# Experts' up products over both parts of the tokens at once, in an encoder layer with a mixture of experts

## Chip, cores and metric

One core of a Trainium2 chip runs one program. The metric is the device time of one execution in microseconds; the times shown are medians of several runs. TensorE (PE) multiplies matrices into PSUM, VectorE (DVE), ScalarE (ACT) and GpSimd (POOL) work beside it, SyncE (SP) issues most of the DMA.

## What is computed

One layer: a normalisation, a projection, neighbourhood attention beside a convolution, an output projection with a residual, then a mixture of 16 experts in which each expert chooses 256 of the 2048 tokens, and a last normalisation. The change is in the experts:

```python
def expert_choice_ffn(h, w_router, w_gate, w_up, w_down):
    logits = jnp.einsum('bsd,de->bse', h, w_router, preferred_element_type=jnp.float32)
    aff = jax.nn.softmax(logits, axis=-1)
    gates, idx = lax.top_k(jnp.swapaxes(aff, 1, 2), cap)      # cap = 256
    xs = h[bidx, idx]
    hid = jax.nn.silu(jnp.einsum('becd,edf->becf', xs, w_gate)) * jnp.einsum('becd,edf->becf', xs, w_up)
    eo = jnp.einsum('becf,efd->becd', hid, w_down)
    return jnp.zeros_like(h).at[bidx, idx].add(gates[..., None].astype(h.dtype) * eo)
```

The model width is 1024, an expert's hidden width 2048, everything is float32.

## The kernel before

A float32 matrix is multiplied as two parts: a high part, which is the value rounded to the matmul's format (fp32r), and a low part, which is what is left. `split` (L122) makes them: ScalarE copies the value into the high part (L123), VectorE subtracts that from the value for the low part (L124). A product of two such matrices is three matmuls, high by high, high by low and low by high; `mm3` issues them one after the other, all through `mm` (L103).

**Experts.** The loop at the end of the kernel goes over 257 chunks. A chunk `jj` is expert `e` and `j` of 16, 128 of the 2048 hidden columns. `up_chunk` makes both up products (`i` = 0 with `w_gate`, 1 with `w_up`) in the two halves of one PSUM bank: for each of 8 slices `d` of the model width, three matmuls whose stationary operand is 128x128 of the weights (`wh` or `wl`) and whose moving operand is one part of the 256 tokens (`xh` or `xl`). `act_chunk` takes Silu of the first half on ScalarE (L1037), multiplies it by the second half on VectorE (L1038), both out of PSUM, and splits the result into `hid`. `down_chunk` multiplies the `hid` of the chunk before by `w_down`, 12 matmuls of 512 columns, into four banks (`accs`) that stay for all 16 chunks of an expert. Behind it stand the jobs of the table `todo`, and then three of the six splits of the next weights, 128x1024 each (`split_part`).

**What stands around it.** The rows of an expert's tokens are gathered by DMA and `turn` transposes them: for `b` = 0 to 3, four transposes (L106) into one bank and a split into the high and the low part of slices 2b and 2b+1. Turns 0 and 1 of the next expert stand in `todo` of an expert's fifteenth chunk, turns 2 and 3 in that of its last, so that they come right ahead of the next expert's first `up_chunk`. In chunks 0 to 26 `todo` also holds the routing of the experts 1 to 15, a search for the affinity of the 256th token: each step takes the last count, offers candidates and reduces on VectorE (L887 to L876), and TensorE counts (a small matmul from `rd`, in the table `early`, between the up products and the down product of the next chunk). One-hot tables (L953) and their lists follow. At an expert's first chunk `finish_expert` scales the sums of the one before (ScalarE L1064, VectorE L1066).

**Order and buffers.** Each engine executes its instructions in the order in which they are written (`manual_schedule`); semaphores stand where one needs another's result or buffer. PSUM has eight banks: four for `accs`, four that rotate. Small tiles of up to 2 KB a partition come from 8 buffers (`e2`), large ones of 8 KB from 22 slots.

Of the kernel before, what the change touches and what calls it, by code (L numbers as in the profile page):

```python
# [9 lines left out]
F32R = mybir.dt.float32r  # L10
BF16 = mybir.dt.bfloat16
I32 = mybir.dt.int32
AF = mybir.ActivationFunctionType
ALU = mybir.AluOpType
AX = mybir.AxisListType

P = 128
# [3 lines left out]
E = 16  # L21
# [33 lines left out]
def kernel(  # L55
# [16 lines left out]
    nc = tc.nc  # L72
# [11 lines left out]
    def uid(s):  # L84
        counter[0] += 1
        return f"{s}{counter[0]}"

    def slot(shape, dt=F32):
        return big.tile(shape, dt, tag="s", name=uid("s"))

    def e2(shape, dt=F32):
        return sm.tile(shape, dt, tag="e2", name=uid("e"))
# [4 lines left out]
    def bank(shape, dt=F32):  # L97
        return psum.tile(shape, dt, tag="b", name=uid("b"))

    pe = [None]  # L100

    def mm(o, l, r, start, stop):
        pe[0] = nc.tensor.matmul(o, l, r, start=start, stop=stop)  # L103

    def tr(o, i, idt):
        pe[0] = nc.tensor.transpose(o, i, idt)  # L106
# [9 lines left out]
    def mm3(o, lh, ll, rh, rl, start, stop):  # L116

        mm(o, lh, rh, start, False)
        mm(o, lh, rl, False, False)
        mm(o, ll, rh, False, stop)  # L120

    def split(hi, lo, src):  # L122
        nc.scalar.activation(hi, src, AF.Copy)  # L123
        nc.vector.tensor_tensor(lo, src, hi.bitcast(F32), op=ALU.subtract)  # L124
# [292 lines left out]
    u = slot([P, T])  # L417
# [13 lines left out]
    for n, (kind, i) in enumerate(jobs):  # L431
# [3 lines left out]
        if kind == "a":  # L435
            u = slot([P, T])
# [333 lines left out]
    for k, b in enumerate((2, 3, 0, 1)):  # L770
        on((98, 106, 112, 118)[k], lambda b=b: wo_load(b))
        for n in range(4):
            i = (104, 109, 115, 121)[k] + n
# [12 lines left out]
    for i in range(-LS, NT_):  # L786
# [5 lines left out]
        j = i + LS  # L792
        if j < NT_:
            h, k = divmod(j, 16)
# [179 lines left out]
    xs_raw, xsT = {}, {}  # L974
# [11 lines left out]

    def turn(e, b):
        if b == 0:
            xsT[e] = (slot([P, 8, 256], F32R), slot([P, 8, 256], F32R))
        hi, lo = xsT[e]  # L990
        ps = bank([P, 2, 256])
        for hf in range(2):
            for j in range(2):
                d = b * 2 + j
                tr(ps[:, j, hf * P : (hf + 1) * P], xs_raw[e][:, hf, d * P : (d + 1) * P], ident)
        split(hi[:, b * 2 : b * 2 + 2], lo[:, b * 2 : b * 2 + 2], ps)


    raw_w, hl_w = {}, {}
# [12 lines left out]
    def split_part(u, part, k):  # L1012

        if k == 0:
            shape = [P, 8, 256] if part < 2 else [P, 2, D]
            hl_w[u, part] = (slot(shape, F32R), slot(shape, F32R))
        split(*(v.rearrange("p a b -> p (a b)")[:, k * 1024 : (k + 1) * 1024] for v in (*hl_w[u, part], raw_w[u, part])))
        if k == 1 and 0 < u < NU - 2:
            load_part(u + 2, part)
# [1 line left out]
    hid = {}  # L1021
    accs = {}

    def up_chunk(e, j):
        u = e * 8 + j // 2
        xh, xl = xsT[e]
        fs = slice((j % 2) * P, (j % 2 + 1) * P)
        ps = bank([P, 2, 256])
        for i in range(2):
            wh, wl = hl_w[u, i]  # L1030
            for d in range(8):
                mm3(ps[:, i], wh[:, d, fs], wl[:, d, fs], xh[:, d], xl[:, d], d == 0, d == 7)
        return ps

    def act_chunk(e, j, ps):
        s = e2([P, 256])
        nc.scalar.activation(s, ps[:, 0], AF.Silu)  # L1037
        nc.vector.tensor_tensor(s, s, ps[:, 1], op=ALU.mult)  # L1038
        h = e2([P, 2, 256], F32R)
        split(h[:, 0], h[:, 1], s)  # L1040
        hid[e, j] = h

    def down_chunk(e, j):
        if j == 0:
            accs[e] = [bank([P, 512]) for _ in range(4)]
        h = hid.pop((e, j))
        wh, wl = hl_w[e * 8 + j // 2, 2]
        for m in range(2):
            ms = slice(m * P, (m + 1) * P)
            for n in range(2):  # L1050
                ns = slice(n * 512, (n + 1) * 512)
                mm3(
                    accs[e][m * 2 + n], h[:, 0, ms], h[:, 1, ms], wh[:, j % 2, ns], wl[:, j % 2, ns],
                    j == 0, j == 15,
                )
# [84 lines left out]
    for b in range(4):  # L1140
        turn(0, b)
# [41 lines left out]
    for e in range(1, E):  # L1183
        j = (e - 1) * 16 + {1: 9, 2: 10}.get(e, 4)
# [7 lines left out]
    for t in range(16):  # L1192
        j = (E - 1) * 16 + 2 + t * 3 // 4
# [4 lines left out]
    for jj in range(E * 16 + 1):  # L1198
        e, j = divmod(jj, 16)
        u = jj // 2  # L1200
        ps = up_chunk(e, j) if e < E else None
        for f in early.pop(jj, []):
            f()
        if e < E:
            act_chunk(e, j, ps)
        if jj:
            down_chunk(*divmod(jj - 1, 16))
            if j == 0 and e < E:
                finish_expert(e - 1)
        if e == E:  # L1210
            break
        for f in todo.pop(jj, []):
            f()
        if u + 1 < NU:
            for p_, k in order[(j % 2) * 3 : (j % 2) * 3 + 3]:
                split_part(u + 1, p_, k)

    e = E - 1
# [114 lines left out]
```

## Time and profile before

| | us |
|---|---|
| median of 3 runs (3258.41 to 3263.06) | 3260.43 |
| the profiled execution | 3264.74 |
| its span, first to last instruction | 3263.0 |
| PE busy (share of the span) | 3137.8 (96%) |
| DVE busy | 2082.9 (64%) |
| ACT busy | 1368.9 (42%) |
| POOL busy | 500.8 (15%) |

The first 1025 us of the span are projections, attention, convolution and the router, the rest are the experts. Matmuls are pipelined: the next starts before one has ended, so that the pace of a stream is read from starts, or from the length of a merged row: its length holds one duration and, for each further matmul, one step of the pace. A row of the order of time merges instructions of one group that follow each other on an engine; a figure in brackets is the idle time ahead of it and what ended it.

### The profile page before, as it was taken

What the parts mean: (1) busy time and instruction counts of PE and PEld (TensorE: products, weight loads), DVE (VectorE), ACT (ScalarE), POOL (GpSimd) and SP (SyncE); (2) the same over time, 40 slices, a digit from 0 to 9 for tenths busy, and PEclk for the clock granted to TensorE, in tenths of its full rate; (3) what the DMA queues carried; (4) which work ended last, traced back from release to release, by engine and by line L of the source; (5) the groups of instructions that cost most, each with busy time, mean ns of one, the idle gap of its engine ahead of it and who ended that gap; (6) DMA issues with size and microseconds to landing.
All of it is one profiled execution on the core that took longest, in us unless ns stands there. A gap on an engine that the chain in (4) does not pass through costs nothing.

```text
span 3263.0 us, 51574 instructions
## 1 busy us (share of the span) xinstructions
PE 3137.8 (96%) x21282; PEld 2880.2 (88%) x21282; DVE 2082.9 (64%) x3229; ACT 1368.9 (42%) x2248; POOL 500.8 (15%) x358
## 2 busy tenths in 40 slices
PE   7999997869997999999999999999999999999998
PEld 6888976767886999999999999999999999999997
DVE  5799966786766787555556555555555555555565
ACT  5111126753333444444444444444444444444454
POOL 2111116665541000000000000000000000000011
PEclk9999998988997999999999999999999999999999
DMA  6231379972334565655656566565665656556585
GB/s 252 59 96 64 121 189 228 225 211 96 124 132 170 203 194 181 212 189 195 205 194 202 191 204 197 188 203 197 198 202 195 195 191 213 189 194 205 194 283 201
DMA packets 392923, 602.51 MB, mean 185 GB/s; under 512 B 13936, under 2 KB 316272, under 8 KB 388976
## 3 DMA queue, kind: packets, MB, share of 16 engines
q1 hardware_dynamic: 357552, 550.91, 51.6%
q0 software_dynamic: 9504, 34.61, 4.2%
q10 hardware_dynamic: 25632, 13.70, 1.4%
q8 instruction: 167, 2.74, 0.3%
q14 instruction: 68, 0.56, 0.1%
HBM read 527.86 MB, written 71.30 MB: 184 GB/s over the span
## 4 chain that ended last, share of the span: by engine, by line
PE 86%; DMA 5%; DVE 5%; issue 2%; POOL 1%; SPq 1%; ACT 0%; POOLq 0%; ACTq 0%; DVEq 0%
PE b L103 83%; DVE s L272 3%; PE b L106 2%; DMA s<-kl_scr 2%; DMA s<-in_tb_dram 1%; DMA s<-v_scr 1%; SPq L110 1%; POOL e L533 0%; POOL s L483 0%; PE b L573 0%; DMA s<-kh_scr 0%; DMA s<-in_xT_dram 0%; DMA gains<-in_rows_dram 0%; DVE s L488 0%; DVE e L124 0%
## 5 line engine op out<-in xcount | busy, mean ns | idle before, releaser
L103 PE MATMUL b<-s,s 128*128 128x256 f32 (+1 forms) x15616 | 2247.5, 302 | 25.9 <-DMA s<-kl_scr 17.5
L103 PEld LDWEIGHTS b<-s,s 128*128 128x128 f32 x15616 | 2073.8, 192 | 138.9 <-issue 18.9
L124 DVE TENSOR_TENSOR s<-s,s 128x1024 fp32r<-128x1024 f32 x768 | 896.3, 1220 | 116.3 <-ACT s L123 106.4
L123 ACT ACTIVATE s<-s 128x1024 fp32r<-128x1024 f32 x768 | 754.8, 1045 | 35.4 <-issue 31.5
L103 PE MATMUL b<-s,e 128*128 128x512 f32 x3072 | 746.7, 392 | 0.0
L103 PEld LDWEIGHTS b<-s,e 128*128 128x128 f32 x3072 | 560.6, 189 | 105.6
L1037 ACT ACTIVATE e<-b 128x256 f32<-128x256 f32 x256 | 98.3, 384 | 986.8 <-PE b L103 986.8
L1038 DVE TENSOR_TENSOR e<-e,b 128x256 f32<-128x256 f32 x256 | 107.7, 421 | 578.4 <-ACT e L1037 578.3
L272 DVE SCALAR_TENSOR_TENSOR s<-s,pv_sb,s 128x2033 f32<-128x2033 f32 (+14 forms) x120 | 310.4, 2587 | 2.0
L1067 POOL DMA_INDIRECT acc<-s,c x30 | 55.7, 1857 | 1251.4 <-ACT s L1064 1141.2
L124 DVE TENSOR_TENSOR e<-e,e 128x256 fp32r<-128x256 f32 x256 | 108.7, 425 | 123.8 <-ACT e L123 123.8
L978 POOL DMA_INDIRECT s<-h_scr,c x32 | 55.7, 1742 | 763.1 <-issue 498.2
L533 POOL TENSOR_SCALAR e<-e,c 128x384 f32<-128x384 f32 (+2 forms) x114 | 143.8, 1269 | 130.5 <-DVE c L531 58.1
L123 ACT ACTIVATE e<-e 128x256 fp32r<-128x256 f32 x256 | 106.9, 417 | 130.0 <-DVE e L1038 130.0
L521 ACT ACTIVATE e<-e,c 128x384 f32<-128x384 f32 (+2 forms) x128 | 79.4, 621 | 92.1 <-DVE c L531 75.0
L573 PE MATMUL b<-s,s 128*128 128x256 f32 (+3 forms) x512 | 96.3, 310 | 18.4 <-DVE s L560 18.2
L573 PEld LDWEIGHTS b<-s,s 128*128 128x128 f32 (+1 forms) x512 | 88.0, 216 | 26.8 <-DVE s L560 22.7
L106 PE MATMUL b<-ident,e 128*96 128x128 f32 (+1 forms) x448 | 81.6, 304 | 30.1 <-POOL e L533 29.9
L517 DVE CUSTOM_DVE_ANT_0 e<-b,s 128x384 f32<-128x384 f32 (+2 forms) x128 | 71.1, 555 | 52.1 <-DMA s<-in_tb_dram 34.7
L124 DVE TENSOR_TENSOR s<-b,s 128x512 fp32r<-128x512 f32 x80 | 52.5, 688 | 70.4 <-ACT s L123 70.3
L106 PEld LDWEIGHTS b<-ident,e 128*96 128x96 f32 (+1 forms) x448 | 52.6, 144 | 41.0 <-POOL e L533 38.5
L560 DVE TENSOR_TENSOR s<-b,s 128x384 fp32r<-128x384 f32 (+3 forms) x128 | 78.3, 612 | 15.9 <-ACT s L555 11.8
(139 smaller groups left out, 1485.3 us busy)
## 6 DMA issues: line engine op xcount, KB each, us to landing
s<-in_w_gate_dram SPq DMA_DIRECT2D x128, 1024.0 KB
s<-in_w_up_dram SPq DMA_DIRECT2D x128, 1024.0 KB
s<-in_w_down_dram SPq DMA_DIRECT2D x128, 1024.0 KB
s<-in_x_dram SPq DMA_DIRECT2D x8, 1024.0 KB
s<-in_xT_dram SPq DMA_DIRECT2D x8, 1024.0 KB
v_scr<-e ACTq DMA_DIRECT2D x32, 256.0 KB
s<-kh_scr SPq DMA_DIRECT2D x16, 512.0 KB
s<-kl_scr SPq DMA_DIRECT2D x16, 512.0 KB
```

What stands on the lines that cost most here:

```text
L103: pe[0] = nc.tensor.matmul(o, l, r, start=start, stop=stop)
L106: pe[0] = nc.tensor.transpose(o, i, idt)
L123: nc.scalar.activation(hi, src, AF.Copy)
L124: nc.vector.tensor_tensor(lo, src, hi.bitcast(F32), op=ALU.subtract)
L272: nc.vector.scalar_tensor_tensor(a[:, s:e], u[:, s + sh : e + sh], tap_w(k), a[:, s:e], op0=ALU.mult, op1=ALU.add)
L517: nc.vector.tensor_tensor_reduce(out=s[:, :n], in0=ps[:, :n], in1=bt[:, boff : boff + n], scale=-1.0, scalar=3.0e38, op0=ALU.add, op1=ALU. ...
L521: nc.scalar.activation(s[:, :n], s[:, :n], AF.Exp, bias=nm[:, rg : rg + 1], scale=-1.0, accum_out=rs_[:, rg : rg + 1])
L533: eng.tensor_scalar(s[:, :n], s[:, :n], ri, None, op0=ALU.mult)
L560: nc.vector.tensor_tensor(lo, src, hi.bitcast(F32), op=ALU.subtract)
L573: nc_mm = nc.tensor.matmul(o[:, r0 : r0 + nr], vt[:nk, g], part[:nk, at : at + nr], start=g == 0 and p == 0, stop=g == 7 and p == 1, skip_ ...
L1037: nc.scalar.activation(s, ps[:, 0], AF.Silu)
L1038: nc.vector.tensor_tensor(s, s, ps[:, 1], op=ALU.mult)
```

## The change

The tokens' parts now lie beside each other: `xsT` is two tiles of four slices each, and in a slice the 256 values of the high part are followed by the 256 of the low part. `up_chunk` makes one of the two up products in a bank of its own. Eight matmuls in a row take a slice of the weights' high part against both parts of the tokens, 512 columns, into both halves of the bank; eight more take the weights' low part against the tokens' high part, 256 columns, into the first half. The new `sum_chunk` adds the halves: ScalarE copies the second into an `e2` tile, VectorE adds the first to it. `act_chunk` then works from these tiles and no longer from PSUM. In `turn` the split writes into strided halves of a tile, with the same number of instructions. The count of columns that TensorE streams is the same.

```diff
     def turn(e, b):
         if b == 0:
-            xsT[e] = (slot([P, 8, 256], F32R), slot([P, 8, 256], F32R))
-        hi, lo = xsT[e]
+
+            xsT[e] = [slot([P, 4, 2, 256], F32R) for _ in range(2)]
+        hi, lo = (xsT[e][b // 2][:, 2 * (b % 2) : 2 * (b % 2) + 2, k] for k in range(2))
...
-        split(hi[:, b * 2 : b * 2 + 2], lo[:, b * 2 : b * 2 + 2], ps)
+        split(hi, lo, ps)
...
-    def up_chunk(e, j):
-        u = e * 8 + j // 2
-        xh, xl = xsT[e]
+    def up_chunk(e, j, i):
+
+        wh, wl = hl_w[e * 8 + j // 2, i]
         fs = slice((j % 2) * P, (j % 2 + 1) * P)
         ps = bank([P, 2, 256])
-        for i in range(2):
-            wh, wl = hl_w[u, i]
-            for d in range(8):
-                mm3(ps[:, i], wh[:, d, fs], wl[:, d, fs], xh[:, d], xl[:, d], d == 0, d == 7)
+        for d in range(8):
+            x2 = xsT[e][d // 4][:, d % 4]
+            nc.tensor.matmul(ps, wh[:, d, fs], x2, start=d == 0, stop=False, skip_group_check=True)
+        for d in range(8):
+            xh = xsT[e][d // 4][:, d % 4, 0]
+            pe[0] = nc.tensor.matmul(ps[:, 0], wl[:, d, fs], xh, start=False, stop=d == 7, skip_group_check=True)
         return ps
 
-    def act_chunk(e, j, ps):
-        s = e2([P, 256])
-        nc.scalar.activation(s, ps[:, 0], AF.Silu)
-        nc.vector.tensor_tensor(s, s, ps[:, 1], op=ALU.mult)
+    def sum_chunk(ps):
+
+        s = e2([P, 2, 256])
+        nc.scalar.activation(s[:, 0], ps[:, 1], AF.Copy)
+        nc.vector.tensor_tensor(s[:, 1], ps[:, 0], s[:, 0], op=ALU.add)
+        return s
+
+    def act_chunk(e, j, g, u):
+        nc.scalar.activation(g[:, 0], g[:, 1], AF.Silu)
+        nc.vector.tensor_tensor(g[:, 0], g[:, 0], u[:, 1], op=ALU.mult)
         h = e2([P, 2, 256], F32R)
-        split(h[:, 0], h[:, 1], s)
+        split(h[:, 0], h[:, 1], g[:, 0])
         hid[e, j] = h
...
-        ps = up_chunk(e, j) if e < E else None
+        if e < E:
+            g = sum_chunk(up_chunk(e, j, 0))
+            u2 = sum_chunk(up_chunk(e, j, 1))
         for f in early.pop(jj, []):
             f()
         if e < E:
-            act_chunk(e, j, ps)
+            act_chunk(e, j, g, u2)
```

How the rows then stand. On TensorE, in the first chunk of expert 0, before: the last slice `d` of the first up product and the first slice of the second. `b_` is the PSUM bank's tile; behind the arrow stand the moving operand (`s_9167` the tokens' high part, `s_9168` their low part) and the stationary one (`s_9046` and `s_9047` the two parts of `w_gate`, `s_9155` and `s_9156` those of `w_up`):

```order
L103 MATMUL b_9205<-s_9167,s_9046 128x256
L103 MATMUL b_9205<-s_9168,s_9046 128x256
L103 MATMUL b_9205<-s_9167,s_9047 128x256
L103 MATMUL b_9205<-s_9167,s_9155 128x256
L103 MATMUL b_9205<-s_9168,s_9155 128x256
L103 MATMUL b_9205<-s_9167,s_9156 128x256
```

The same chunk now, the whole of both up products (here `s_9167` and `s_9168` are slices 0 to 3 and 4 to 7, each with both parts):

```order
L1032 MATMUL b_9205<-s_9167,s_9046 128x512 x4
L1032 MATMUL b_9205<-s_9168,s_9046 128x512 x4
L1035 MATMUL b_9205<-s_9167,s_9047 128x256 x4
L1035 MATMUL b_9205<-s_9168,s_9047 128x256 x4
L1032 MATMUL b_9225<-s_9167,s_9155 128x512 x4
L1032 MATMUL b_9225<-s_9168,s_9155 128x512 x4
L1035 MATMUL b_9225<-s_9167,s_9156 128x256 x4
L1035 MATMUL b_9225<-s_9168,s_9156 128x256 x4
```

Forty-eight matmuls of 256 columns became 16 of 512 and 16 of 256, the low parts of all slices are read within the first eight, and the second product has a bank of its own.

On VectorE, in a chunk of the routing stretch, before: the multiply, the low part of `hid`, the routing step from the last count (`kf`) to the reduction (`rd`) that TensorE counts next, and the weights' splits:

```order
L1038 TENSOR_TENSOR e_11139<-e_11139,b_11088 128x256
L124 TENSOR_TENSOR e_11142<-e_11139,e_11142 128x256
L887 TENSOR_SCALAR kf_11157<-b_11137 128x42
L890 TENSOR_REDUCE kp_11159<-kf_11157 128x14
L891 SCALAR_TENSOR_TENSOR thr_9204<-kp_11159,thr_9204 128x14
L863 TENSOR_SCALAR lv_11162<-levels 128x3
L865 TENSOR_TENSOR cd_11164<-thr_9204,lv_11162 128x42
L870 TENSOR_TENSOR e_11166<-aff,cd_11164 128x672
L876 TENSOR_REDUCE rd_11168<-e_11166 128x42
L124 TENSOR_TENSOR s_11085<-s_10785,s_11084 128x1024
L124 TENSOR_TENSOR s_11175<-s_10793,s_11174 128x1024 x2
```

Such a chunk now:

```order
L1042 TENSOR_TENSOR e_10915<-b_10898,e_10915 128x256
L1042 TENSOR_TENSOR e_10935<-b_10918,e_10935 128x256
L1047 TENSOR_TENSOR e_10915<-e_10915,e_10935 128x256
L124 TENSOR_TENSOR e_10942<-e_10915,e_10942 128x256
L887 TENSOR_SCALAR kf_10957<-b_10938 128x42
L890 TENSOR_REDUCE kp_10959<-kf_10957 128x14
L891 SCALAR_TENSOR_TENSOR thr_9204<-kp_10959,thr_9204 128x14
L863 TENSOR_SCALAR lv_10962<-levels 128x3
L865 TENSOR_TENSOR cd_10964<-thr_9204,lv_10962 128x42
L870 TENSOR_TENSOR e_10966<-aff,cd_10964 128x672
L876 TENSOR_REDUCE rd_10968<-e_10966 128x42
```

Two additions from PSUM stand ahead of the multiply, which no longer reads PSUM itself; all that follows comes two instructions later in VectorE's queue.

On ScalarE, in the same kind of chunk, before (Silu, the high part of `hid`, the weights' splits):

```order
L1037 ACTIVATE e_11139<-b_11088 128x256
L123 ACTIVATE e_11142<-e_11139 128x256
L123 ACTIVATE s_11084<-s_10785 128x1024
L123 ACTIVATE s_11174<-s_10793 128x1024 x2
L1037 ACTIVATE e_11233<-b_11182 128x256
```

And now:

```order
L1041 ACTIVATE e_10915<-b_10898 128x256
L1041 ACTIVATE e_10935<-b_10918 128x256
L1046 ACTIVATE e_10915<-e_10915 128x256
L123 ACTIVATE e_10942<-e_10915 128x256
L123 ACTIVATE s_10894<-s_10625 128x1024
L123 ACTIVATE s_10974<-s_10633 128x1024 x2
```

Two copies from PSUM came ahead of Silu, and Silu reads a tile of SBUF.

## Rows read from the trace of the kernel before

**Rows 1.** The page: busy us, share of the span, instructions of each engine.
```profile
PE 3137.8 (96%) x21282; PEld 2880.2 (88%) x21282; DVE 2082.9 (64%) x3229; ACT 1368.9 (42%) x2248; POOL 500.8 (15%) x358
```
**Rows 2.** Windows, columns in the first row: the experts' stage; a routing chunk; another chunk.
```profile
core 0: us, PE busy (x) PEld busy (x) DVE busy (x) ACT busy (x) POOL busy (x), PEclk, DMA share, GB/s
1600.00:1800.00 200.00, 200.00 (x1467) 188.11 (x1467) 111.73 (x164) 88.48 (x123) 13.28 (x7) 1.00 0.62 203
...
1222.80:1231.40 8.60, 8.60 (x63) 8.07 (x62) 7.22 (x13) 3.65 (x5) 0.00 (x0) 1.00 0.48 154
...
1608.50:1617.00 8.50, 8.50 (x61) 8.01 (x61) 4.43 (x5) 3.80 (x6) 0.00 (x0) 1.00 0.74 196
```
**Rows 3.** Order of time, TensorE: start us, length us, engine, line, operation, tiles, shape, count.
```profile
2024.99 5.92 PE L103 MATMUL b<-s,s 128*128 128x256 f32 x48
2030.74 2.91 PE L103 MATMUL b<-s,e 128*128 128x512 f32 x12
2033.49 5.92 PE L103 MATMUL b<-s,s 128*128 128x256 f32 x48
```
**Rows 4.** Order of time, TensorE, narrow stretches: up, down (two), projections (two).
```profile
2024.99 5.68 PE L103 MATMUL b<-s,s 128*128 128x256 f32 x46
...
2031.90 1.75 PE L103 MATMUL b<-s,e 128*128 128x512 f32 x7
...
2030.74 1.32 PE L103 MATMUL b<-s,e 128*128 128x512 f32 x5
...
155.61 7.59 PE L103 MATMUL b<-s,s 128*128 128x512 f32 x31
...
149.72 6.05 PE L103 MATMUL b<-s,s 128*128 128x512 f32 x26
```
**Rows 5.** One line's instructions by shape: duration ns min/median/max, first and last start.
```profile
L103 PE MATMUL b<-s,s x15616: 277/283/796, 17.8 to 3242.1; 128*128 128x256 f32 x164, 128*128 128x512 f32 x31, 128*128 128x384 f32 x2, 128*128 128x288 f32 x1
L103 PE MATMUL b<-s,e x3072: 387/389/478, 1037.4 to 3247.5; 128*128 128x512 f32 x192
...
L124 DVE TENSOR_TENSOR s<-b,s x80: 680/691/694, 747.5 to 3109.8; 128x512 fp32r<-128x512 f32 x80
```
**Rows 6.** Groups from 1100 to 3250 us: busy us, mean ns | idle before, releaser.
```profile
L1038 DVE TENSOR_TENSOR e<-e,b 128x256 f32<-128x256 f32 x247 | 103.9, 421 | 558.5 <-ACT e L1037 558.4
...
L1037 ACT ACTIVATE e<-b 128x256 f32<-128x256 f32 x247 | 94.9, 384 | 948.5 <-PE b L103 948.5
```
**Rows 7.** Order of time at an expert's first chunk: the up product, the turns' low parts.
```profile
1999.41 4.80 PE L103 MATMUL b<-s,s 128*128 128x256 f32 x38
...
1999.88 1.29 DVE L124 TENSOR_TENSOR s<-b,s 128x512 fp32r<-128x512 f32 x2 [2.07 <-ACT s L123]
```
**Rows 8.** Order of time in a routing chunk: VectorE's round and TensorE's count.
```profile
1222.47 0.42 DVE L1038 TENSOR_TENSOR e<-e,b 128x256 f32<-128x256 f32 x1 [0.72 <-ACT e L1037]
...
1226.11 0.85 DVE L876 TENSOR_REDUCE rd<-e 128x42 bf16<-128x672 bf16 x1
...
1226.88 3.48 DVE L124 TENSOR_TENSOR s<-s,s 128x1024 fp32r<-128x1024 f32 x3
...
1230.47 0.19 PE L103 MATMUL b<-rd,small 128*128 128x42 bf16 x1
...
1231.08 0.42 DVE L1038 TENSOR_TENSOR e<-e,b 128x256 f32<-128x256 f32 x1 [0.72 <-ACT e L1037]
```
**Rows 9.** Order of time at expert 1's first chunk.
```profile
1163.77 1.80 PE L103 MATMUL b<-s,s 128*128 128x256 f32 x13
...
1165.09 1.28 DVE L124 TENSOR_TENSOR s<-b,s 128x512 fp32r<-128x512 f32 x2
...
1165.82 2.33 PEld L103 LDWEIGHTS b<-s,s 128*128 128x128 f32 x19 [0.46 <-DVE s L124]
```

## Prediction

> **What bounds the kernel now.** I read the page's busy shares first: TensorE is busy for 96% of the span, VectorE for 64%, ScalarE for 42% [rows 1]. Such shares are means over unlike stages, so the windows came next. In the experts' stage TensorE is busy for 200.00 us of every 200 at a granted clock of 1.00, that is 2.4 GHz, while VectorE has 112 and ScalarE 88 [rows 2]. Nothing but TensorE's own stream sets the time there, and a change of that stage is worth what it takes from the stream plus whatever wait it creates. The order of time gives the stream's beat: the 48 matmuls of a chunk's up products start at 2024.99, the 12 of the down product at 2030.74, the next chunk's at 2033.49 [rows 3]. So a chunk is 5.75 us up and 2.75 us down, and there are 256 chunks.
>
> **The price of one matmul.** A row of a narrow stretch gives the pace: its length less one matmul's own duration, over the number of matmuls less one. Forty-six of 256 columns take 5.68 us; with 283 ns for one, the pace is (5.68 - 0.283)/45 = 119.9 ns. Seven of 512 columns take 1.75 us; with 389 ns for one, (1.75 - 0.389)/6 = 226.8 ns [rows 4, 5]. At 2.4 GHz the columns alone are 106.7 and 213.3 ns. Both kinds therefore pay some 13 ns beside their columns, so one matmul of 512 is 13.0 ns cheaper than two of 256 (239.8 - 226.8).
> The page "TensorE: Matmul & The Clock Gate" of the Trainium skill, section "Back-to-back issue gap", gives N/2.4 + 2.5 ns for an isolated gap, 109 and 216 ns here; the trace disagrees, with 119.9 and 226.8. By the page a merge would return 2.5 ns and not 13, in all 16 x 256 x 2.5 ns = 10.2 us, an estimate from the page that the waits worked out below would eat; the mechanism by which that could come true is the second rival.
>
> **Up products.** Of a product's 24 matmuls of 256 columns, 16 become 8 of 512 and 8 stay. The columns are the same (16 x 512 + 16 x 256 = 48 x 256); the matmuls of a chunk fall from 48 to 32, the weight loads with them. Without disturbance a chunk's up products cost 16 x 226.8 + 16 x 119.9 = 5547 ns in place of 5750, less some 14 ns since the first 256 behind a 512 follows sooner than its pace (48 x 119.9 is 5755, the rows have 5750; I take 7 ns for each such place, an estimate). That gives 5533 ns: 217 ns a chunk, **55.6 us** over 256.
>
> **Taking the sums out of PSUM.** Each product now needs a ScalarE copy and a VectorE add of 128x256 from PSUM: two of each per chunk. The nearest rows are the Silu from PSUM, 384 ns, and the multiply from PSUM, 421 ns [rows 6]. ScalarE gets 0.77 us more per chunk on 3.7, VectorE 0.84 us more on 4.4, of a chunk of 8.3 us [rows 2]. That time is hidden. What is not hidden is that such reads slow the matmuls beside them: the first five of a down product, beside Silu and multiply, take 1.32 us, (1.32 - 0.389)/4 = 232.8 ns in place of 226.8; over the five that is some 28 ns [rows 4]. The reads of the up sum fall on the down product as before; those of the gate sum fall on the first five 512s of the up product, and are new: 28 ns x 256 = **7.2 us** back. Bounds: nothing, or twice that if the reads reach further into the product.
> The page "PSUM — Partial Sum Buffer" of the skill, section "Specifications (TRN2)", says that ScalarE and VectorE can read PSUM in parallel at full bandwidth as long as no bank collides. It speaks of these two, not of TensorE's writes; read as covering them it would leave the 7.2 us out. The trace disagrees: the reads are of another bank and the matmuls still go from 226.8 to 232.8.
>
> **Latency of a chunk's hidden part.** Behind the last up product stood Silu, multiply, copy, subtraction. Now stand copy, add, multiply, copy, subtraction, with Silu beside the add: one add, 0.42 us, later. The down product of that chunk is issued one chunk later, some 6 us after this is done, so it costs nothing. The banks: four are held by the down sums, four rotate, so a sum's bank is needed again two chunks later when no routing counts rotate with them. No wait there.
>
> **An expert's first chunk.** Here the order of the matmuls costs something. The last two turns (transposes of the gathered rows) stand right ahead of it on TensorE. Its matmuls start at 1999.41; VectorE's two subtractions that make the low parts of d = 4, 5 and of d = 6, 7 run from 1999.88 for 1.29 us, so they are done some 1.16 (one takes 691 ns) and 1.76 us after the start [rows 5, 7]. Before, the low part of d = 4 is read by the 14th matmul, 13 x 0.12 = 1.56 us in, of d = 6 by the 20th, 2.28 us in: just early enough. After, every one of the first eight matmuls streams both parts: the fifth, due at 0.91, waits 0.3 us with the semaphore, the seventh, due 0.45 later at 1.66, waits 0.15. That is 0.45 us for each of experts 2 to 15: **6.3 us** (bounds 0.2 and 0.9 each: 3 to 13).
>
> **The routing stretch (chunks 0 to 26).** VectorE also searches the other experts' thresholds here, and is busy for 7.22 of 8.60 us [rows 2]. Its round from one multiply (1222.47) to the end of the last split (1226.88 + 3.48 = 1230.36) is 7.89 us, with 0.72 us idle before the next [rows 8]. Two adds make it 8.73, and TensorE's round falls from 8.61 to 8.42. VectorE so falls behind by 0.31 us a chunk. Who waits: TensorE's count of the candidates, which needs VectorE's reduction. That ends at 1226.96, the count runs at 1230.47, 3.5 us later; less the add and the faster round, 2.9 us are left. By chunk 15 some 2.5 us of lag are there (six chunks at 0.31, the rest from the one-hot tables of chunks 9 and 10, an estimate). It meets expert 1's first product: there the two subtractions start at 1165.09 and end at 1166.37, and TensorE's loads stand idle for 0.46 us already [rows 9]. The first ends 2.0 us after the product's start (1163.77); plus add and lag, 4.9, against 0.91 due: 4.0 + 0.15 us, where some 0.5 is paid now: +3.7. The wait lets VectorE catch up; the second ten routing chunks and expert 0's finish (two scalings of 0.75) make 4.6 us of lag against 2.9 of slack: +1.7. **5.4 us** (bounds: 2 if the lag is absorbed, 9 if the chunks before lag too).
>
> **Sum.** -55.6 + 7.2 + 6.3 + 5.4 = -36.7 us. The profiled execution took 3264.7 us (span 3263.0 and 1.7 around it), 4.3 above the median of 3260.4; the terms are far larger than that 0.13%, so they go on the median: **3224 us**. Its own range: all bounds good give 3260.4 - 55.6 + 3 + 2 = 3210; all bad give 3260.4 - 55.6 + 14.4 + 13 + 9 = 3241.
>
> **Rivals.**
> 1. *VectorE becomes the bound of more than the routing.* If its lag never drains in chunks 0 to 26 (27 x 0.31 = 8.4, tables, turns and finish 6: 14 us) and the turns of each expert come 1 us later behind the longer queue (14 + 6.3 more), then -55.6 + 7.2 + 14 + 20 = -14: 3246, between 3241 and 3256. For it: 7.22 of 8.60 in the routing. Against it: 4.4 of 8.5 elsewhere.
> 2. *The 512s give nothing back, and the time ends above before.* In the projections' stage 31 matmuls of 512 columns take 7.59 us, (7.59 - 0.389)/30 = 240.0 ns each [rows 4]: two 256s' worth. At that pace a chunk's up products save 5750 - (16 x 240.0 + 16 x 119.9 - 14) = 6 ns, 1.5 us in all, against 6.3 + 5.4 of waits and 7.2 of reads: 3278. It decides from a mean pace of 235.8: 9.0 ns more on each of 16 x 256 is 36.9 us, the whole sum. Against it: those 31 stream q's tokens through a permuted view, while 26 others of that stage on plain rows take 6.05 us, 226.4 each [rows 4]; the new ones read 512 neighbours, and the down product's hold 226.8 beside ScalarE's copies. The page's 2.5 ns would give, by the same waits, 3260.4 - 10.2 + 18.9 = 3269.
> 3. *It gives more:* no read disturbs and VectorE's slack absorbs the waits, 3260.4 - 55.6 = 3205.
>
> **How the numbers follow.** Forecast 0.74; rival 1 0.12; rival 2 0.08; rival 3 0.06. A measurement of this kernel tells about 0.2% (6.5 us) from no change. Faster: the forecast, rival 3 and three quarters of rival 1, 0.89; same: the rest of rival 1 and a quarter of rival 2, 0.05; slower: 0.06. The range 3206 to 3247 takes in the forecast's own and half of rivals 1 and 3; it leaves out rival 2 and the rest, under 2 in 10.
>
> **What would show it.** An ordinary chunk of 8.31 us (up 5.56, down 2.75) in the order of time, 512s at 227 to 233 ns; TensorE still at 200 of 200 from 1300 us on but for a gap of under half a microsecond ended by VectorE at each expert's start; waits of TensorE on VectorE of some microseconds at expert 1's start. The forecast is wrong if the 512s of the up products run at 236 or more, if TensorE waits in ordinary chunks, or if the granted clock falls behind one of the new waits.

## The result, and the profile after

The changed kernel takes 3224.51 us (median of 4 runs, 3222.12 to 3225.69) beside 3259.42 us before on the same chip: ratio 0.989, interval 0.9875 to 0.9906, that is 31 to 41 us less. Forecast were 3224 us.

The page of the changed kernel, first its engines (to [rows 1]), then the groups that are new; columns as on the page of before:

```profile
PE 3094.5 (96%) x17186; PEld 2659.5 (83%) x17186; DVE 2275.4 (71%) x3741; ACT 1536.8 (48%) x2760; POOL 499.4 (16%) x358
...
L1032 PE MATMUL b<-s,s 128*128 128x512 f32 x4096 | 1032.4, 393 | 4.4 <-DVE s L124 3.3
...
L1035 PE MATMUL b<-s,s 128*128 128x256 f32 x4096 | 572.9, 283 | 1.9 <-DVE s L124 1.9
L1041 ACT ACTIVATE e<-b 128x256 f32<-128x256 f32 x512 | 195.7, 382 | 739.6 <-PE b L1035 689.6
L1042 DVE TENSOR_TENSOR e<-b,e 128x256 f32<-128x256 f32 x512 | 212.8, 421 | 366.3 <-ACT e L1041 366.2
```

TensorE has 4096 matmuls fewer (21282 - 17186, 16 in each of 256 chunks), and the copies and adds take 382 and 421 ns, where [rows 6] has 384 and 421 for the Silu and the multiply from PSUM. VectorE's share rose from 64% to 71%.

An ordinary chunk in the order of time on TensorE (start us, length us, ..., count), to hold against [rows 3]:

```profile
2029.69 1.98 PE L1032 MATMUL b<-s,s 128*128 128x512 f32 x8
2031.50 1.12 PE L1035 MATMUL b<-s,s 128*128 128x256 f32 x8
2032.46 2.00 PE L1032 MATMUL b<-s,s 128*128 128x512 f32 x8
2034.30 1.11 PE L1035 MATMUL b<-s,s 128*128 128x256 f32 x8
2035.25 2.91 PE L103 MATMUL b<-s,e 128*128 128x512 f32 x12
2038.00 0.96 PE L103 MATMUL b<-tables,s 128*128 128x5 bf16 x32
```

From 2029.69 to 2035.25 are the up products, 5.56 us in place of 5.75, and to 2038.00 the down product, 2.75 as before: a chunk of 8.31 in place of 8.50 us. And TensorE hardly waits there; from 1300 to 3100 us (columns as in [rows 2], PE busy first):

```profile
1300.00:3100.00 1800.00, 1799.24 (x9941) 1546.46 (x9942) 1181.53 (x1836) 958.53 (x1563) 98.50 (x56) 1.00 0.62 202
```

Over the whole stage, from the starts of the down products (the first matmul of each in the order of time) of chunks 0, 27 and 254; one profiled execution each, all in us; the last column is the usual time from one down product to the next. The routing lies in the first stretch, the expert starts 2 to 15 in the second. The names are those of the experiments below. One execution of e8_grouped took 7837.81 us, more than twice any other, and is left out of its figures.

| kernel | first down product at | chunk 0 to 27 | chunk 27 to 254 | ordinary chunk |
|---|---|---|---|---|
| before | 1037.4 | 237.8 | 1967.0 | 8.500 |
| changed | 1027.9 | 240.7 | 1931.0 | 8.307 |
| e1_two_256 | 1031.0 | 242.5 | 1970.7 | 8.500 |
| e2_no_sums | 1032.8 | 233.0 | 1932.7 | 8.307 |
| e3_turns_early | 1031.4 | 237.6 | 1925.4 | 8.307 |
| e4_pool_split | 1027.8 | 251.7 | 1931.1 | 8.307 |
| e5_both | 1031.8 | 252.7 | 1924.5 | 8.307 |
| e6_low_second | 1031.4 | 243.9 | 1927.5 | 8.307 |
| e7_low_pool | 1032.0 | 268.9 | 1927.6 | 8.307 |
| e8_grouped | 1033.1 | 238.9 | 1927.6 | 8.287 |
| e9_four_switches | 1031.0 | 240.7 | 1936.1 | 8.354 |
| e10_mixed | 1029.2 | 237.1 | 1926.1 | 8.287 |
| e11_best | 1030.1 | 235.4 | 1923.0 | 8.287 |

What the second column times is, but for the up products of the first two chunks (under half a microsecond), work that no kernel here changes; it varies by up to 9.6 us between these executions, so a span of one profile says less than the two stretches. (TensorE's waits for one load of the attention, `kl_scr`, alone are 17.5 us in the profile of before and 11.2 in that of the changed kernel.) The stretches say +2.9 and -36.0: the change gains 36 us in the experts, and loses 3 in the routing, where 27 chunks should have gained 27 x 0.193 = 5.2.

What is lost in the routing. Two stretches of the order of time of the changed kernel: chunk 18's second up product, and expert 1's first chunk (16):

```profile
1178.24 0.85 DVE L876 TENSOR_REDUCE rd<-e 128x42 bf16<-128x672 bf16 x1
...
1179.01 3.48 DVE L124 TENSOR_TENSOR s<-s,s 128x1024 fp32r<-128x1024 f32 x3
1179.03 0.63 PE L1035 MATMUL b<-s,s 128*128 128x256 f32 x4
1180.28 0.54 PEld L1035 LDWEIGHTS b<-s,s 128*128 128x128 f32 x4 [0.82 <-DVE s L124]
...
1155.15 0.85 DVE L876 TENSOR_REDUCE rd<-e 128x42 bf16<-128x672 bf16 x1
1155.92 1.28 DVE L124 TENSOR_TENSOR s<-b,s 128x512 fp32r<-128x512 f32 x2
1156.66 0.30 PEld L1032 LDWEIGHTS b<-s,s 128*128 128x128 f32 x2 [3.73 <-DVE s L124]
1156.66 1.33 PE L1032 MATMUL b<-s,s 128*128 128x512 f32 x4 [3.31 <-DVE s L124]
```

In chunk 18 four of the second product's 256s run, then TensorE waits until the first of VectorE's three splits is done: it is the second half of `w_up`'s low part, split in the odd chunk ahead. Chunks 14, 20, 22 and 24 wait too, some 0.6 us each. (From the start of down product k to the next run the up products of chunk k + 2. The expectations number waits by k: their chunk 12 is 14 here.) At expert 1's start the fifth 512 waits 3.31 us for a turn's low part, which stands behind the routing's reduction. And the wait has a second price. Windows of 2 us behind it (columns in the first row, the granted clock after POOL):

```profile
core 0: us, PE busy (x) PEld busy (x) DVE busy (x) ACT busy (x) POOL busy (x), PEclk, DMA share, GB/s
...
1156.00:1158.00 2.00, 1.34 (x6) 0.95 (x7) 2.00 (x4) 0.27 (x1) 0.00 (x0) 1.00 1.09 417
1158.00:1160.00 2.00, 2.00 (x10) 1.90 (x10) 2.00 (x3) 0.38 (x1) 0.00 (x0) 0.51 0.73 301
1160.00:1162.00 2.00, 2.00 (x7) 1.51 (x7) 0.94 (x2) 0.00 (x0) 0.00 (x0) 0.63 0.00 0
1162.00:1164.00 2.00, 2.00 (x15) 1.78 (x14) 0.25 (x1) 0.67 (x2) 0.00 (x0) 1.00 0.00 0
```

TensorE was idle for 3.3 us, started again at 1156.66, and from about 1158 ran at 1.2 GHz for some 3.4 us: the windows from 1158 and 1160 lack 0.49 and 0.37 of full speed, 2 x 0.86 = 1.7 us of work, which at half speed is 3.4 us. Of the chunk's 14.60 us, 5.3 stand above 8.43 and its two turns (0.88, as 9.38 - 8.50 in the later experts of before): 3.3 and 0.3 of waits, and 1.7 us of clock. The fall of the clock is not certain behind such a wait: in e8_grouped the same wait, 3.33 us, was followed by none (granted 1.00 from 1150 to 1170 us), and the chunk took 13.07 us.

An expert's start in the later experts (order of time, changed kernel), to [rows 7]:

```profile
1298.82 2.55 PE L1032 MATMUL b<-s,s 128*128 128x512 f32 x8
...
1299.30 1.29 DVE L124 TENSOR_TENSOR s<-b,s 128x512 fp32r<-128x512 f32 x2 [1.54 <-ACT s L123]
...
1300.04 0.30 PEld L1032 LDWEIGHTS b<-s,s 128*128 128x128 f32 x2 [0.48 <-DVE s L124]
1300.64 0.30 PEld L1032 LDWEIGHTS b<-s,s 128*128 128x128 f32 x2 [0.30 <-DVE s L124]
```

Eight 512s take 2.55 us where an ordinary product has 1.98, and 2.07 right behind transposes when nothing is late (at 1291.91 in e3_turns_early). TensorE's weight loads, which run one matmul ahead, stand idle for 0.48 and 0.30 us.

### The profile page after: what moved, and what is told of

It is laid out like the page before. It is cut to its first block, busy times and chain, and to the rows that moved or that the text cites. A ratio compares the mean times of both kernels' runs of the same rounds, so it can differ in the third digit from the quotient of the medians.

```text
span 3220.3 us, 44621 instructions
## 1 busy us (share of the span) xinstructions
PE 3094.5 (96%) x17186; PEld 2659.5 (83%) x17186; DVE 2275.4 (71%) x3741; ACT 1536.8 (48%) x2760; POOL 499.4 (16%) x358
## 3 DMA queue, kind: packets, MB, share of 16 engines
q10 hardware_dynamic: 25632, 13.70, 1.4%
## 4 chain that ended last, share of the span: by engine, by line
PE 81%; DVE 9%; DMA 5%; issue 2%; POOL 1%; ACT 1%; SPq 0%; POOLq 0%; ACTq 0%; DVEq 0%
PE b L103 37%; PE b L1032 27%; PE b L1035 14%; DVE s L272 3%; PE b L106 2%; DVE s L124 2%; DMA s<-in_tb_dram 2%; DMA s<-kl_scr 1%; DVE e L870 1%; DMA kl_scr<-e 0%; POOL e L533 0%; DMA s<-v_scr 0%; DVE e L124 0%; POOL s L483 0%; PE b L573 0%
## 5 line engine op out<-in xcount | busy, mean ns | idle before, releaser
L1032 PE MATMUL b<-s,s 128*128 128x512 f32 x4096 | 1032.4, 393 | 4.4 <-DVE s L124 3.3
L1032 PEld LDWEIGHTS b<-s,s 128*128 128x128 f32 x4096 | 748.4, 189 | 157.0 <-DVE s L124 15.0
L103 PE MATMUL b<-s,s 128*128 128x512 f32 (+3 forms) x3328 | 725.8, 371 | 19.1 <-DMA s<-kl_scr 11.2
L103 PEld LDWEIGHTS b<-s,s 128*128 128x128 f32 x3328 | 567.3, 192 | 114.7 <-issue 12.6
L1035 PEld LDWEIGHTS b<-s,s 128*128 128x128 f32 x4096 | 559.5, 190 | 43.2 <-DVE s L124 3.0
L1035 PE MATMUL b<-s,s 128*128 128x256 f32 x4096 | 572.9, 283 | 1.9 <-DVE s L124 1.9
L1041 ACT ACTIVATE e<-b 128x256 f32<-128x256 f32 x512 | 195.7, 382 | 739.6 <-PE b L1035 689.6
L1042 DVE TENSOR_TENSOR e<-b,e 128x256 f32<-128x256 f32 x512 | 212.8, 421 | 366.3 <-ACT e L1041 366.2
L1047 DVE TENSOR_TENSOR e<-e,e 128x256 f32<-128x256 f32 x256 | 108.9, 426 | 28.1 <-ACT e L1046 4.1
L1046 ACT ACTIVATE e<-e 128x256 f32<-128x256 f32 x256 | 104.7, 409 | 38.0 <-DVE e L1042 37.7
```

Source lines behind the costliest of these rows:

```text
L1032: nc.tensor.matmul(ps, wh[:, d, fs], x2, start=d == 0, stop=False, skip_group_check=True)
L1035: pe[0] = nc.tensor.matmul(ps[:, 0], wl[:, d, fs], xh, start=False, stop=d == 7, skip_group_check=True)
L1041: nc.scalar.activation(s[:, 0], ps[:, 1], AF.Copy)
L1042: nc.vector.tensor_tensor(s[:, 1], ps[:, 0], s[:, 0], op=ALU.add)
L1046: nc.scalar.activation(g[:, 0], g[:, 1], AF.Silu)
L1047: nc.vector.tensor_tensor(g[:, 0], g[:, 0], u[:, 1], op=ALU.mult)
```

## Experiments

Theory at the outset: each matmul pays some 13 ns beside its columns, which is the gain; the reads of PSUM for the sums slow the 512s beside them; the low parts come late at expert starts; VectorE's queue is late in the routing. One rival for each.

**One part undone: the 512s as pairs of 256 (e1_two_256).**

```diff
-            nc.tensor.matmul(ps, wh[:, d, fs], x2, start=d == 0, stop=False, skip_group_check=True)
+            for k in range(2):
+                nc.tensor.matmul(ps[:, k], wh[:, d, fs], x2[:, k], start=d == 0 and k == 0, stop=False, skip_group_check=True)
```

> The changed kernel with each matmul of 512 columns issued as two of 256 with the same stationary operand; banks, sums and order stay. Theory (each matmul pays some 13 ns beside its columns): 16 more matmuls in each chunk, a chunk back from 8.31 to 8.50 us, no 512 in the up products for the PSUM reads to slow; 0.19 x 256 = 49 us more, less 2 to 4 us of waits in the routing, where a longer chunk gives VectorE time: 3269 to 3273 us. Rival (the gain comes from the new order, in which a weight slice is changed less often): no change, 3224 us.

Measured: 3265.95 us, ratio to before 1.0028 (1.0018 to 1.0039). From the page (to [rows 1]), and the order of time on TensorE:

```profile
PE 3143.3 (96%) x21282; PEld 2883.0 (88%) x21282; DVE 2275.1 (70%) x3741; ACT 1536.1 (47%) x2760; POOL 501.6 (15%) x358
...
2302.79 2.08 PE L1033 MATMUL b<-s,s 128*128 128x256 f32 x16
2304.70 1.12 PE L1036 MATMUL b<-s,s 128*128 128x256 f32 x8
2305.66 2.08 PE L1033 MATMUL b<-s,s 128*128 128x256 f32 x16
2307.59 1.12 PE L1036 MATMUL b<-s,s 128*128 128x256 f32 x8
2308.55 2.91 PE L103 MATMUL b<-s,e 128*128 128x512 f32 x12
```

Up products of 2308.55 - 2302.79 = 5.76 us, the chunk at 8.500 again. So the gain is the number of matmuls, and the new order alone brings nothing. Each matmul comes with its own weight load: there are 21282 of both again, though the second load of a pair brings the same slice again. How much of the 13 ns is the load's and how much the matmul's, no run here separates. (2.08 - 0.283)/15 = 119.8 ns a pair's half, as in [rows 4]. What is left of the change without its merge, the sums and the earlier reading of the tokens' low parts, costs 0.28%, some 9 us: 4.7 in the first stretch and 3.7 in the second of the table.

**The sums left out (e2_no_sums).** Silu and multiply read the first halves of the banks.

```diff
     def sum_chunk(ps):
-        s = e2([P, 2, 256])
-        nc.scalar.activation(s[:, 0], ps[:, 1], AF.Copy)
-        nc.vector.tensor_tensor(s[:, 1], ps[:, 0], s[:, 0], op=ALU.add)
-        return s
+        return ps
...
-        nc.scalar.activation(g[:, 0], g[:, 1], AF.Silu)
-        nc.vector.tensor_tensor(g[:, 0], g[:, 0], u[:, 1], op=ALU.mult)
+        s = e2([P, 256])
+        nc.scalar.activation(s, g[:, 0], AF.Silu)
+        nc.vector.tensor_tensor(s, s, u[:, 0], op=ALU.mult)
...
```

> The changed kernel without the sums: Silu and multiply read the first half of each bank, so the product of the weights' high part and the tokens' low part is computed and left out of the result. Theory (the sums cost the PSUM reads beside the second up product and VectorE's lag in the routing): the second product's 512s at 227 ns throughout, an ordinary chunk of 8.28 us, 7 us less over 256 chunks; the waits of chunks 10 to 26, 8 us in the profile, mostly gone: 3209 us, with expert starts still waiting. Rival (the sums are hidden, the waits come from the order of the products alone): 3222 to 3225 us.

Measured: 3216.86 us, ratio 0.9872 (0.9855 to 0.9888), against 0.989 of the changed kernel. The routing's part came as expected: 233.0 us from chunk 0 to 27, 7.7 less than with the sums, and TensorE waits for VectorE there once, 0.5 us. So the routing's waits are the sums' time in VectorE's queue. But the ordinary chunk stayed at 8.307 us, where the theory had 8.28. Order of time, second up product and down product:

```profile
2311.05 2.00 PE L1032 MATMUL b<-s,s 128*128 128x512 f32 x8
2311.25 0.38 ACT L1043 ACTIVATE e<-b 128x256 f32<-128x256 f32 x1 [2.63 <-PE b L1035]
...
2312.89 1.11 PE L1035 MATMUL b<-s,s 128*128 128x256 f32 x8
...
2313.84 1.32 PE L103 MATMUL b<-s,e 128*128 128x512 f32 x5
2314.11 0.42 DVE L1044 TENSOR_TENSOR e<-e,b 128x256 f32<-128x256 f32 x1 [1.62 <-PE b L1035]
```

VectorE no longer reads PSUM beside the second up product, ScalarE none beside the down product, and still the eight 512s take 2.00 us and the first five of the down product 1.32, as in [rows 4]. It fell to the next runs to say what the 28 ns are.

**The low part second (e6_low_second).** One 512, eight 256s, seven 512s.

```diff
-        for d in range(8):
-            x2 = xsT[e][d // 4][:, d % 4]
-            nc.tensor.matmul(ps, wh[:, d, fs], x2, start=d == 0, stop=False, skip_group_check=True)
+        def both(d):
+            x2 = xsT[e][d // 4][:, d % 4]
+            pe[0] = nc.tensor.matmul(ps, wh[:, d, fs], x2, start=d == 0, stop=d == 7, skip_group_check=True)
+
+        both(0)
         for d in range(8):
             xh = xsT[e][d // 4][:, d % 4, 0]
-            pe[0] = nc.tensor.matmul(ps[:, 0], wl[:, d, fs], xh, start=False, stop=d == 7, skip_group_check=True)
+            nc.tensor.matmul(ps[:, 0], wl[:, d, fs], xh, start=False, stop=False, skip_group_check=True)
+        for d in range(1, 8):
+            both(d)
```

> The changed kernel with the up product's order changed: the first slice's 512, then the eight 256s, then seven 512s. Theory (PSUM reads slow the 512s and leave the 256s alone, and the tokens' low parts of slices 4 to 7 are needed later): an ordinary chunk of 8.28 us, 7 us less over 256; no wait at expert starts, 6.7 us less; but the weights' low part is read 1.6 us earlier, which in the routing's chunks gives back up to 9 us: 3211 to 3220 us. Rival (the slow 512s are slow for another reason than the reads, such as being first in a bank): ordinary chunk still 8.31 us.

Measured: 3223.69 us, ratio 0.9895 (0.9878 to 0.9911): no gain, and the chunk at 8.307, which is what the rival had. Order of time of a chunk's first up product, then of its second and of the down product, with what reads PSUM beside the latter (L1045 and L1046, the sums' copy and add):

```profile
2306.26 2.00 PE L1032 MATMUL b<-s,s 128*128 128x512 f32 x8
...
2309.05 1.78 PE L1032 MATMUL b<-s,s 128*128 128x512 f32 x7
2310.67 2.88 PE L103 MATMUL b<-s,e 128*128 128x512 f32 x12
...
2310.87 0.38 ACT L1045 ACTIVATE e<-b 128x256 f32<-128x256 f32 x1 [2.41 <-PE b L1032]
2311.15 0.41 ACT L1050 ACTIVATE e<-e 128x256 f32<-128x256 f32 x1
2311.28 0.42 DVE L1046 TENSOR_TENSOR e<-b,e 128x256 f32<-128x256 f32 x1 [1.13 <-ACT e L1045]
```

The down product has both readers beside it and runs at (2.88 - 0.389)/11 = 226.5 ns, undisturbed; it now stands behind 512s. The first product's seven, behind the 256s, start where nothing reads PSUM (the gate sum's copy is at 2308.07, its add at 2309.74), and with the second product's first they take (2.00 - 0.389)/7 = 230.1; the second product's seven, with that add beside them, (1.78 - 0.389)/6 = 231.8, and single steps are the same in both within 1 ns. So the reads are not the cause. The theory put in its place: **behind a run of 256s the first five 512s are slow** (233, 236, 228, 233 and 231 ns from start to start, 28 ns above five of 226.7), and the first 256 behind a 512 is followed after 113 and not 120.

The rest of this run: the starts of experts 2 to 15 cost 0.42 us less each (9.25 in place of 9.67 us for such a chunk), but the routing lost 3.2 us, since the weights' low parts are read 1.6 us sooner, and the last expert's chunks some 2 us.

**The number of switches.** Once in a chunk (e8_grouped):

```diff
...
+        for i in range(2):
+            for d in range(8):
+                x2 = xsT[e][d // 4][:, d % 4]
+                nc.tensor.matmul(pss[i], w[i][0][:, d, fs], x2, start=d == 0, stop=False, skip_group_check=True)
+        for i in range(2):
+            for d in range(8):
+                xh = xsT[e][d // 4][:, d % 4, 0]
+                pe[0] = nc.tensor.matmul(pss[i][:, 0], w[i][1][:, d, fs], xh, start=False, stop=d == 7, skip_group_check=True)
...
```

> The changed kernel with both products' 512s first and both products' 256s behind them: the stream goes from 256 to 512 columns once in a chunk and not twice. Theory (the first five 512s behind a 256 are slow, 28 ns together, whoever reads PSUM, and the first 256 behind a 512 is 7 ns early): an ordinary chunk of 8.286 us in place of 8.307, 5 us less in all, about 0.9875 of before. Rival (the reads of PSUM slow the 512s beside them): the down product's first five, beside the up sum's reads, stay slow in either case; the gate sum's reads now fall on 256s, 8.28 us; so this run does not tell the two apart, the next one does.

Measured: 3218.26 us (median of three runs), ratio 0.9879 (0.9859 to 0.9898), the chunk at 8.287. And four times (e9_four_switches):

```diff
-        for d in range(8):
-            x2 = xsT[e][d // 4][:, d % 4]
...
+        for q in range(2):
+            for d in range(4 * q, 4 * q + 4):
+                x2 = xsT[e][d // 4][:, d % 4]
+                nc.tensor.matmul(ps, wh[:, d, fs], x2, start=d == 0, stop=False, skip_group_check=True)
+            for d in range(4 * q, 4 * q + 4):
+                xh = xsT[e][d // 4][:, d % 4, 0]
+                pe[0] = nc.tensor.matmul(ps[:, 0], wl[:, d, fs], xh, start=False, stop=d == 7, skip_group_check=True)
```

> The changed kernel with each product as four 512s, four 256s, four 512s, four 256s: four switches from 256 to 512 in a chunk with the same sums and reads. Theory (the switch costs): 21 ns more for each of two further switches (28 less the early 256), an ordinary chunk of 8.35 us, 11 us more, less 3 to 4 us of waits at the expert starts, where the low parts are read 0.48 us later: some 3231 us, 0.991 of before. Rival (the reads cost): 8.31 us, and 3221 us for the shorter waits.

Measured: 3228.28 us, ratio 0.9907 (0.9891 to 0.9924), the chunk at 8.354. Order of time, first with one switch, then with four:

```profile
2315.78 2.08 PE L1037 MATMUL b<-s,s 128*128 128x256 f32 x16
2317.70 2.91 PE L103 MATMUL b<-s,e 128*128 128x512 f32 x12
2320.44 3.79 PE L1033 MATMUL b<-s,s 128*128 128x512 f32 x16
```

```profile
2306.66 1.07 PE L1033 MATMUL b<-s,s 128*128 128x512 f32 x4
2307.57 0.64 PE L1036 MATMUL b<-s,s 128*128 128x256 f32 x4
2308.04 1.09 PE L1033 MATMUL b<-s,s 128*128 128x512 f32 x4
```

Behind the down product's 512s sixteen more run at (3.79 - 0.389)/15 = 226.7 ns; behind 256s four take 1.09 and not 1.07 us. One, two and four switches give 8.287, 8.307 and 8.354 us: 20 and some 23 ns each, and 28 less 7 is 21. The mechanism inside TensorE was not looked into; that the switch costs, and the reads do not, is shown.

**Turns one chunk earlier (e3_turns_early).**

```diff
-            at(e * 16 - 2 + b // 2, lambda e=e, b=b: turn(e, b))
+            at(e * 16 - 3 + b // 2, lambda e=e, b=b: turn(e, b))
```

> The changed kernel with all four turns of the next expert one chunk earlier. Theory (each expert's first chunk waits for the low parts of slices 4 to 7): the 0.48 us of each of 14 starts go, 6.7 us, and at expert 1's start the long wait becomes a short one for the weights: 3 us; 3215 us. Rival (the wait only stands in for another that is due at the same place, such as the weights' low parts): 3222 us or more.

Measured: 3217.16 us, ratio 0.9875 (0.9858 to 0.9891). Both stretches of the table gained, 3.1 and 5.6 us. An expert's first product, which now stands right behind a down product:

```profile
1297.57 2.91 PE L103 MATMUL b<-s,e 128*128 128x512 f32 x12
1300.32 1.98 PE L1032 MATMUL b<-s,s 128*128 128x512 f32 x8
```

1.98 us as in any chunk, no wait. Expert 2 pays 0.9 us for it, since its rows are gathered only one chunk ahead and the turns then wait for the gather. At expert 1 the long wait went, and with it the slow clock; the lag came out as 1.2 and 1.0 us more in chunks 14 and 18.

**GpSimd for the third split of chunks 0 to 26 (e4_pool_split).**

```diff
...
-            for p_, k in order[(j % 2) * 3 : (j % 2) * 3 + 3]:
-                split_part(u + 1, p_, k)
+            for n, (p_, k) in enumerate(order[(j % 2) * 3 : (j % 2) * 3 + 3]):
+                split_part(u + 1, p_, k, nc.gpsimd if n == 2 and jj < 27 else None)
```

> The changed kernel with the third split's subtraction of each of the chunks 0 to 26 on GpSimd. Theory (VectorE's queue is late in the routing by 0.31 us a chunk): 1.13 us of VectorE's round of 8.7 go, no lag is left, the waits of 0.6 us in chunks 12 to 22 vanish and that at expert 1's start shrinks from 4.8 to 1.5 us: 3218 us. Rival (GpSimd's 3.5 us per subtraction comes too late for TensorE or slows VectorE beside it): 3224 us or more.

Measured: 3235.77 us, ratio 0.9937 (0.992 to 0.9953): 11 us lost in the first stretch, the rival's side. Groups from 1015 to 1300 us, first of this run, then of the changed kernel:

```profile
L124 POOL TENSOR_TENSOR s<-s,s 128x1024 fp32r<-128x1024 f32 x27 | 70.9, 2635 | 161.4 <-ACT s L123 145.9 <-ACT e L1041 6.0 <-DVE s L124 5.7
...
L124 DVE TENSOR_TENSOR s<-s,s 128x1024 fp32r<-128x1024 f32 x63 | 108.3, 1761 | 0.7 <-ACT s L123 0.5
```

```profile
L124 DVE TENSOR_TENSOR s<-s,s 128x1024 fp32r<-128x1024 f32 x93 | 108.1, 1218 | 0.7 <-ACT s L123 0.5
```

VectorE does 30 subtractions fewer in the same 108 us (27 are GpSimd's, three fall behind the window): one of its own takes 1761 ns in the mean and not 1218. A multiply of 0.43 us (at 1125.09) took 2.84 beside one of GpSimd's of 2.41, so it stood still for all of that. The Trainium skill's page "SBUF — State Buffer", section "Who interferes with whom", says so: a VectorE instruction with two SBUF inputs contends with a GpSimd instruction that reads SBUF. The trace agrees. Of the 11 us, some 7.5 are further waits of TensorE for VectorE (12.7 us from 1015 to 1300, and 5.2 in the changed kernel); the rest is its clock, granted at half for 10.2 us here and for 3.4 there.

The same with the earlier turns (e5_both), and with the low part second (e7_low_pool):

> Turns one chunk earlier and the third split's subtraction of chunks 0 to 26 on GpSimd, together. Theory: the two waits are separate and add: 6.7 us at 14 expert starts and some 8 us in the routing, 3209 to 3211 us. Rival (one hides the other): no better than the better one alone, 3215 us.

> That order and the third split's subtraction of chunks 0 to 26 on GpSimd. Theory: 7 us for the reads, 6.7 us at the expert starts and 6 to 8 us in the routing: 3203 to 3207 us, the best of all. Rival (the weights' low part then comes late in the routing): 3211 us or more.

Measured: 3231.06 us, ratio 0.9918 (0.9901 to 0.9934), and 3250.82 us, ratio 0.9978 (0.9968 to 0.9988). GpSimd takes all of the gain of the turns in the first stretch (252.7 us, the second still at 1924.5), and with the low parts read earlier yet TensorE waits 20.0 us for VectorE there.

**The old form where VectorE is busy (e10_mixed).** Chunks 0 to 25 as before the change, the rest grouped, turns of experts 3 to 15 earlier:

```diff
...
+        if jj < 26:
+            ps = up_old(e, j)
+        elif e < E:
+            pss = up_pair(e, j)
+            g, u2 = sum_chunk(pss[0]), sum_chunk(pss[1])
...
-            at(e * 16 - 2 + b // 2, lambda e=e, b=b: turn(e, b))
+            at(e * 16 - (3 if e > 2 else 2) + b // 2, lambda e=e, b=b: turn(e, b))
```

> Chunks 0 to 25 in the old form (sums in PSUM, no copies and adds), the others grouped as in e8_grouped, and the turns of experts 3 to 15 one chunk earlier. Theory: the routing's chunks cost what they cost before, 237.8 us from chunk 0 to 27 in place of 240.7; 20 ns x 228 chunks = 5 us for the switch; 0.48 x 13 = 6 us for the expert starts: 3210 to 3212 us, 0.985 of before. Rival (other waits take their place): 3217 us or more.

Measured: 3214.08 us, ratio 0.9866 (0.9849 to 0.9882). The first stretch has 237.1 us, as expected. In the second, 13.70 us for chunk 244 in this profile were not: there TensorE waits 3.64 us for ScalarE's split, and ScalarE 4.05 for a load of the last norm that stands ahead in its queue; behind it the granted clock fell once more. Hence the last run (e11_best), its edit against e10_mixed:

```diff
-        if jj < 26:
+        if 10 <= jj < 26:
...
-        at(j + 1, lambda t=t: final_norm(t))
-        at(j + 2, lambda t=t: final_store(t))
+        at(min(j + 2, E * 16 - 1), lambda t=t: final_norm(t))
+        at(min(j + 3, E * 16 - 1), lambda t=t: final_store(t))
```

> As e10_mixed, with the old form in chunks 10 to 25 alone, where the routing's larger search runs, and with the last norm's square and scaling one chunk later behind their load, so that ScalarE does not stand before a row that has not landed. Theory: 0.2 us for each of ten more chunks, 2 us; the waits of the last expert's chunks 2 to 8 (5.4 and 1.1 us in the profile of e10_mixed) gone, in as far as other executions have them: 3205 to 3210 us, 0.984 of before. Rival (the last expert's waits come from the queue of loads, which more rows in flight lengthen): 3212 us or more.

Measured: 3213.79 us, ratio 0.9866 (0.985 to 0.9883). The ten chunks brought 1.7 us (235.4); the last expert's waits moved to other chunks (9.30 and 10.55 us for 248 and 252) and the end behind the last down product takes 20.0 us in place of 18.0, so the total is on the rival's side, and those waits are not solved. Both versions are below the kernel before, and their medians some 10 us below the changed one; their intervals touch that one's.

## Why the prediction was right, step by step

- **The price of one matmul: right.** 119.9 and 226.8 ns carried over to products that the trace of before did not have, and undoing the merge gave 8.500 us back.
- **55.6 us less 7.2: right in size, wrong in cause.** The chunk of 8.31 us was forecast and measured, but the 28 ns were put on PSUM reads of the sums. They belong to the change from 256 to 512 columns: two a chunk now, one before. The prediction's reading that reads of another bank slow the matmuls does not hold: the down product of e6_low_second keeps 226.5 ns beside both. In [rows 4] both stood at the same place, the first five 512s of the down product, so that the trace of before could not tell them apart. The mistaken cause also carried two expectations that failed, 8.28 us without the sums and with the low part second.
- **Nothing for the copies and adds in ordinary chunks: right.** From 1300 to 3100 us TensorE is busy for 1799.24 of 1800.00 us.
- **Expert starts, 0.45 us each: right.** A chunk with such a start takes 9.67 us in place of 9.38 - 0.19, 0.48 us each, 6.7 in all; 6.3 were forecast. With the turns earlier the wait is gone, so the late low parts are the cause.
- **The routing, 5.4 us: too small.** The stretch cost 240.7 - (237.8 - 5.2) = 8.1 us, within the bounds of 2 to 9. That VectorE's queue is the cause held: without the sums it is 0.4. The step that failed is who waits. Named was TensorE's count; in the trace the low half of `w_up`'s next unit is due first, from chunk 14 on, and the slack of 2.9 us was worked out for the wrong waiter. At expert 1's start 3.7 us were forecast and 4.8 measured (14.60 - 10.00 + 0.19). Of these, 1.7 are the slow clock behind the wait, which the prediction had as a sign of being wrong and gave no price: in this profile that sign is there.
- **The sum: -36.7 forecast, -34.9 between the medians.** In the two profiles the experts' stage alone gained 33.1 us; the 0.193 us of 254 chunks, 49.0, less 6.7, less 8.1 and some 1 us of waits in the last expert. That the median fell on the forecast to the microsecond is partly luck: the gain came out 1.8 us smaller than forecast and the median of before 1.0 us lower than the one it was taken from, and the first 1025 us of the span vary by more than that.
- **The rivals.** The 512s did not lose their pace (rival 2; (1.98 - 0.389)/7 = 227 ns in the first product); VectorE's lag stayed in the routing (rival 1); and the waits were not absorbed (rival 3), 6.7 and 8.1 us. The isolated gap of 2.5 ns beside the columns that the Trainium skill's page "TensorE: Matmul & The Clock Gate", section "Back-to-back issue gap", states would have ended at 3269 us by the prediction's estimate; the runs here show some 13.

## What to carry to other kernels

Where TensorE's stream is the bound, count its matmuls and not only their columns: here two of 256 columns cost 13 ns more than one of 512, each with its own weight load, and a fusion that saves them is worth that times its count. Then look where the engine that pays for it (here VectorE, with two adds a chunk) is nearly full in one stage, keep the old form there, and find the waiter by which operand of TensorE's next matmuls is finished last, not by which wait the code names.

## What the runs showed of the hardware

- The first five 512-column matmuls behind a run of 256-column ones start 233, 236, 228, 233 and 231 ns apart and not 226.7, and the first 256 behind a 512 is followed after 113 and not 120 ns: 20 to 23 ns for a switch there and back, with or without readers of PSUM beside it.
- A VectorE multiply of two SBUF tiles stood still for the 2.41 us of a GpSimd subtraction of 128x1024; with a third of the splits on GpSimd, VectorE's time for the others was 108.3 us, and 108.1 for all.
- An idle gap of 3.31 us in TensorE's stream was followed by some 3.4 us at a granted clock of half, 1.7 us lost, at which 512 columns took 427 ns from start to start; a gap of 3.33 us at the same place in e8_grouped was followed by no fall, one of 2.92 in e1_two_256 was.
